# A state-space recurrence handled two chunks at a visit instead of one, between the projections of a hybrid layer

## The chip, the cores and the metric

The kernel runs on one core of a Trainium2 chip. The metric is the device time of one execution in microseconds (us), as the median of several runs. The core has five engines that work side by side: TensorE for matrix products (PE in the profile, with PEld for the loading of its weights), VectorE (DVE), ScalarE (ACT), GpSimd (POOL) and SyncE (SP), which here only issues transfers (DMA). Products land in PSUM, a small memory of eight banks; everything else lies in SBUF, the working memory. A bank holds 512 single-precision numbers for each of 128 partitions.

## The reference

One layer, 1024 positions of 1024 channels, in single precision: a normalisation, one large projection into ten parts, two branches on the parts, gates, an output projection and a last normalisation. The change lies in the first branch, a chunked recurrence (SSD) with 16 heads in 4 groups and chunks of 128 positions, so 8 chunks to a group:

```python
xdt = (xs * dt[..., None]).reshape(bsz, nc, q, g, r, p)
da_cs = jnp.cumsum((dt * a).reshape(bsz, nc, q, g, r), axis=2)
...
decay = jnp.exp(jnp.where(causal[None, None, :, :, None, None], seg, -jnp.inf))
cb = jnp.einsum('bclgn,bcsgn->bclsg', cc, bc)
y_diag = jnp.einsum('bclsgr,bcsgrp->bclgrp', cb[..., None] * decay, xdt)
to_end = jnp.exp(da_cs[:, :, -1:] - da_cs)
states = jnp.einsum('bcsgn,bcsgrp->bcgrpn', bc, xdt * to_end[..., None])
...
def step(carry, inp):
    st, dec = inp
    return carry * dec[..., None, None] + st, carry
...
y_off = jnp.einsum('bclgn,bcgrpn->bclgrp', cc, prev) * jnp.exp(da_cs)[..., None]
y = (y_diag + y_off).reshape(bsz, seqlen, n_heads, p)
```

Within a chunk the output is `y_diag`, a masked product. Across chunks a state of 128 by 64 numbers for each head is carried along, and `y_off` is what the state before a chunk adds to that chunk's output.

## The kernel before

**The stream of projections.** Nearly all of PE's time goes into projections and output products. Each takes two column blocks of weights as a `Pair` (L325 to L460) and computes them by seven products of half size instead of eight, in the manner of Strassen. One such product is a *step*: 12 matmuls of 128 by 128 on 128 by 512, half of which is a *half* (`Stream.half`, L563). The steps of all 48 pairs stand in one fixed list (L501 to L517). For each step, ACT and DVE split the weights into a high and a low part (`split`, L350, which writes the tile `wop`), three steps ahead of the product. Between products 1, 6 and 7 of a pair the partial sum in a bank is copied out by ACT (`keep`, L407), into one of three buffers of the tag `s`, and DVE later adds it to or subtracts it from another product (`give`, L413, at L420, L422 and L424). Products 1, 6, 7 and 4 of a pair add up in one bank (`pb`), so product 4 can't begin before copy 7 is taken.

**The recurrence.** Other work is laid between the halves: a generator does some of it, then yields a number of halves that the stream is to do (`beside`, L638). `ssd(g)` (L850) is the generator of one group's recurrence. Its parts for a chunk `c`:

- `sums(c)` (L855) loads the running sums of the decays, spread over all partitions, into `csb` (128 by 512, two buffers).
- `decays(c)` (L884) makes, on ACT, four clipped differences (L891) and one exponential (L895) into `m4` (`m` in the profile).
- `first(c)` (L861) is two to three transposes and the product `cb`, all into a bank `tr`; from that DVE makes `xdt` (L872) and the causal `cbm` (L877), ACT copies `bn` (L880), and DVE multiplies the decays by `cbm` (L882): the masked decays.
- `more(c)` (L897): on POOL `xe` (L904); the exponential of the sums into a tile `ce` of its own, on ACT (L910), which POOL multiplies by `ct` (L911).
- `second(c)` (L913) is the state's product `st` (two records of 256 columns in the profile, since a single-precision product counts as two), the new state (POOL L925, DVE L929), and the output products into the bank `yps`: for each of two tiles and two heads first the masked decays against `xdt`, then, for c > 0, the scaled `ct` against the state before. These have 64 columns of output; the profile has them as 128*64. After each odd chunk DVE adds the bank to `xs` (L943).

A visit for chunk c (L959 to L978) is `second(c)`, `first(c+1)`, `more(c+1)`, the load for c+3, then 2 halves of the stream, `decays(c+2)`, and 2 more halves.

**What orders the work.** All matmuls, transposes and everything under `pin` stay in the order in which the program writes them, each engine for itself. Other instructions are put in order when the program is built, by a priority that goes by program order and by when their inputs should be there; `tc.high_priority()` moves an instruction up. After that, every engine works strictly through its list. A tile of a tag with n buffers waits, when it is first written, until the tile n before it (of that tag) is read for the last time.

**Other users of the same buffers.** The setup of the decays (`dt_and_f`, L693), the group's gates and norm (`gate_and_norm`, L1007) and its two halves of `squares` (L980) borrow `csb`, `ce` and `m4` between groups. `turn_values` (L824) transposes a part of the attention's values, when at least 2 halves have gone since it was made.

Of the kernel before, what the change touches and what calls it, by code (L numbers as in the profile page):

```python
# [86 lines left out]
def hybrid_layer(ctx: ExitStack, tc, a, out):  # L87
# [237 lines left out]
    class Pair:  # L325
# [7 lines left out]
        def __init__(self, keys, handlers, ops=None, adds=nc.vector):  # L333
            self.keys, self.handlers = keys, handlers
            self.ops = xop if ops is None else ops
            self.adds = adds
            self.raw, self.op, self.prepared = {}, {}, set()
            self.s1, self.sums = None, 0

# [67 lines left out]
        def keep(self, ps):  # L407
            s = wp.tile([P, HALF], F32, tag="s", bufs=3, name="s")
            with tc.high_priority():
                nc.scalar.activation(s, ps, AF.Copy)  # L410
            return s
# [15 lines left out]
        def do(self, which):  # L427
# [4 lines left out]
            if which == 1:  # L432
# [3 lines left out]
                self.k1 = self.keep(self.b)  # L436
# [5 lines left out]
            elif which == 6:  # L442
                yield from self.matmuls(self.b, 6, "-t2", False)
                self.k2 = self.keep(self.b)
            elif which in (5, 7):
# [3 lines left out]
                else:  # L449
                    yield from self.matmuls(self.b, 7, "t3", False)  # L450
                    self.k7 = self.keep(self.b)
# [241 lines left out]
    def dt_and_f():  # L693

        def rows(tag, bufs):
# [4 lines left out]
            sp.tile([P, 4, P], F32, tag="csb", bufs=2, name="t").rearrange("p a b -> p (a b)") for _ in range(2)  # L700
# [62 lines left out]
        fc = [rows("ce", 1), rows("csb", 2)]  # L763
# [86 lines left out]
    def ssd(g):  # L850
# [4 lines left out]
        def sums(c):  # L855

            if c < NT:
                csb = at[c]["csb"] = sp.tile([P, 4, P], F32, tag="csb", bufs=2, name="csb")
                nc.sync.dma_start(csb, cs_dram[hs, c * P : (c + 1) * P].unsqueeze(0).to_broadcast([P, 4, P]))

        def first(c):  # L861
# [14 lines left out]
            cbm = sp.tile([P, P], F32, tag="cbm", bufs=1, name="cbm")  # L876
            nc.vector.tensor_tensor(cbm, tr[:, 3 * P :], tri, ALU.mult)  # L877
            if c < NT - 1:
                bn = s["bn"] = sp.tile([P, P], F32, tag="bn", bufs=1, name="bn")
                nc.scalar.activation(bn, tr[:, 2 * P : 3 * P], AF.Copy)  # L880
            m4 = s["m4"]
            nc.vector.tensor_tensor(m4, m4, cbm.unsqueeze(1).to_broadcast([P, 4, P]), ALU.mult)  # L882

        def decays(c):  # L884

            if c < NT:
                csb = at[c]["csb"]
                m4 = at[c]["m4"] = sp.tile([P, 4, P], F32, tag="m4", bufs=2, name="m4")
                for h in range(4):
                    pin(  # L890
                        nc.scalar.activation(  # L891
                            m4[:, h, :], csb[:, h, :], AF.Relu, scale=-1.0, bias=cscol[:, c, 4 * g + h : 4 * g + h + 1]
                        )
                    )
                pin(nc.scalar.activation(m4, m4, AF.Exp, scale=-1.0))  # L895

        def more(c):  # L897

            cs = slice(c * P, (c + 1) * P)
            s = at[c]  # L900
            if c < NT - 1:
                xe = s["xe"] = sp.tile([P, 4, 64], F32, tag="xe", bufs=1, name="xe")
# [4 lines left out]
                )  # L907
            if c > 0:
# [4 lines left out]
        def second(c, prev, yps):  # L913

            s = at[c]
            new = None
            if c < NT - 1:
                st = pp.tile([P, 4, 64], F32, tag="st", bufs=1, name="st")
                mm(st, s["bn"], s["xe"], start=True, stop=True)
                new = sp.tile([P, 4, 64], F32, tag="prev", bufs=3, name="new")  # L920
                if c == 0:
                    nc.vector.tensor_copy(new, st)
                else:
                    pin(
                        nc.gpsimd.tensor_tensor(  # L925
                            new, prev, cdec[:, c, hs].unsqueeze(2).to_broadcast([P, 4, 64]), ALU.mult
                        )
                    )
                    nc.vector.tensor_tensor(new, new, st, ALU.add)  # L929
            cc = slice((c % 2) * P, (c % 2 + 1) * P)  # L930
            for j in range(2):
                for e in range(2):
                    h = 2 * j + e
                    mm(yps[e * 64 : e * 64 + 64, j, cc], s["xdt"][:, h, :], s["m4"][:, h, :], start=True, stop=(c == 0))
                if c > 0:
                    for e in range(2):
                        h = 2 * j + e
                        mm(yps[e * 64 : e * 64 + 64, j, cc], prev[:, h, :], s["ce"][:, h, :], start=False, stop=True)
            if c % 2 == 1:
                c2 = slice((c - 1) * P, (c + 1) * P)  # L940
                for j in range(2):
                    i = 2 * g + j
                    nc.vector.scalar_tensor_tensor(  # L943
                        xs[j][:, c2], xs[j][:, c2], dsk[:, i : i + 1], yps[:, j, :], ALU.mult, ALU.add
                    )
            return new

        prev = yps = early = None
        sums(0)
        sums(1)  # L950
        yield 2
        decays(0)
        yield 2
        first(0)
        more(0)
        sums(2)
        decays(1)
        yield 4
        for c in range(NT):  # L959
            if c % 2 == 0:  # L960
                yps = pp.tile([P, 2, 2 * P], F32, tag="y", bufs=1, name="yps")
            prev = second(c, prev, yps)
            if c + 1 < NT:
                first(c + 1)
                more(c + 1)
            sums(c + 3)
            if c == 4:
# [4 lines left out]
                next(early)  # L972
            elif early:
                next(early, None)
            turn_values()
# [760 lines left out]
```

## Time and profile before

| | |
|---|---|
| three runs | 1292.45, 1295.67, 1298.04 us; median 1295.67 |
| the profiled execution | 1295.78 us |
| its span, first to last instruction | 1294.1 us |
| granted TensorE clock, mean | 0.997 |
| busy: PE, DVE, ACT, POOL | 1253.6, 1017.4, 794.1, 289.1 us |
| the recurrence of the four groups, in us from the span's start | 130 to 188, 266 to 325, 402 to 464, 545 to 604 |
| DMA: moved, mean rate | 233.59 MB, 181 GB/s |

How to read the lines that follow. A timeline row has the start in us, the length, the engine, the line of the kernel, the operation, the tiles written and read, and how many such instructions the row merges; in brackets stands how long the engine had been idle, and who ended that. A row of a group has a count, then busy time in us, the mean ns of one, and the idle time ahead of it. The end of a matmul is modelled, so neighbouring matmuls overlap in the rows; what PE really takes is read from one start to the next. "raw" is a block of weights, "th" a buffer for results on their way out, "pb", "pc" and "pd" are the banks of the projections.

### The profile page before, as it was taken

Reading aid. Unit: us, or ns where it says so; the run is one execution under the profiler, and the core shown is the slowest. Engines: PE = TensorE matmul, PEld = TensorE weight load, DVE = VectorE, ACT = ScalarE, POOL = GpSimd, SP = SyncE. Lnnn points to the kernel's source line nnn. Section 1 sums busy time; section 2 is a strip of 40 time slices with the busy share of each in tenths; the row PEclk is TensorE's granted clock in tenths of the full one; section 3 lists DMA queues with packets and bytes.
Section 4 is the critical chain, followed back from the end, with each engine's and each line's share of the span. In section 5 each row is a group of like instructions: output and inputs, shape, how many; then the busy total and the mean of one; then the engine's idle time right before and its main releaser. Section 6 shows DMA issues by size and latency. Waiting matters only on the chain. (4 is left out here: it accounts for less than half of the span.)

```text
span 1294.1 us, 21088 instructions
## 1 busy us (share of the span) xinstructions
PE 1253.6 (97%) x7066; PEld 987.1 (76%) x7066; DVE 1017.4 (79%) x1979; ACT 794.1 (61%) x1729; POOL 289.1 (22%) x307
## 2 busy tenths in 40 slices
PE   6999999999999999899999999999999999999997
PEld 4787888788887788688777777777767777678786
DVE  6999888798789879788666666666789778877875
ACT  8745666477556656566556666566677656743754
POOL 0000430034102420143001222222121313246052
PEclk9999999999999999999999999999999999999999
DMA  7332453654463444454464656566687657666932
GB/s 281 102 107 83 144 149 120 199 144 144 128 209 120 146 154 159 126 151 155 164 230 164 212 180 225 191 214 204 220 278 252 220 176 262 222 212 195 363 117 97
DMA packets 154668, 233.59 MB, mean 181 GB/s; under 512 B 17216, under 2 KB 62656, under 8 KB 154560
## 3 DMA queue, kind: packets, MB, share of 16 engines
q1 hardware_dynamic: 142016, 205.53, 50.0%
q0 software_dynamic: 6400, 16.10, 3.3%
q10 hardware_dynamic: 6144, 10.62, 2.2%
q8 instruction: 55, 0.90, 0.3%
q14 instruction: 53, 0.43, 0.1%
HBM read 162.99 MB, written 72.34 MB: 182 GB/s over the span
## 5 line engine op out<-in xcount | busy, mean ns | idle before, releaser
L356 DVE TENSOR_TENSOR wop<-sum,wop 128x512 fp32r<-128x512 f32 x174 | 140.3, 807 | 55.0 <-ACT wop L354 54.4
L354 ACT ACTIVATE wop<-sum 128x512 fp32r<-128x512 f32 x174 | 108.8, 626 | 91.8 <-DVE sum L363 39.0
L1502 ACT ACTIVATE ex<-ex,nm 128x512 f32<-128x512 f32 (+1 forms) x192 | 116.1, 606 | 73.0 <-DVE nm L1498 72.2
L410 ACT ACTIVATE s<-pb 128x512 f32<-128x512 f32 x141 | 83.4, 592 | 95.2 <-PE pb L130 93.1
L356 DVE TENSOR_TENSOR wop<-raw,wop 128x512 fp32r<-128x512 f32 x149 | 107.1, 721 | 33.9 <-ACT wop L354 33.4
L130 PE MATMUL pc<-x3h,wop 128*128 128x512 f32 x384 | 130.2, 397 | 3.2 <-ACT wop L354 2.1
L130 PE MATMUL pb<-x0h,wop 128*128 128x512 f32 x384 | 131.4, 399 | 0.1
L130 PE MATMUL pc<-x2h,wop 128*128 128x512 f32 x384 | 130.2, 398 | 0.0
L130 PE MATMUL pb<-x6h,wop 128*128 128x512 f32 x376 | 127.7, 397 | 1.6 <-ACT s L410 1.6
L130 PE MATMUL pb<-x5h,wop 128*128 128x512 f32 x376 | 127.0, 396 | 1.3 <-ACT s L410 1.3
L130 PE MATMUL pb<-x4h,wop 128*128 128x512 f32 x376 | 127.4, 397 | 0.3 <-DVE wop L356 0.3
L1498 DVE CUSTOM_DVE_ANT_0 ex<-s,fb 128x512 f32<-128x512 f32 (+1 forms) x192 | 96.7, 552 | 23.5 <-PE s L130 23.4
L354 ACT ACTIVATE wop<-raw 128x512 fp32r<-128x512 f32 x151 | 93.8, 623 | 14.8 <-PE pc L130 9.9
L130 PEld LDWEIGHTS pc<-x3h,wop 128*128 128x128 f32 x384 | 72.2, 188 | 20.8 <-ACT wop L354 3.0
L130 PE MATMUL pd<-x1h,wop 128*128 128x512 f32 x264 | 87.7, 393 | 0.0
L130 PEld LDWEIGHTS pb<-x0h,wop 128*128 128x128 f32 x384 | 72.7, 189 | 16.6 <-ACT x0h L1218 0.8
L130 PEld LDWEIGHTS pb<-x6h,wop 128*128 128x128 f32 x376 | 70.7, 188 | 17.8 <-ACT s L410 2.5
L130 PEld LDWEIGHTS pc<-x2h,wop 128*128 128x128 f32 x384 | 72.1, 188 | 15.9 <-DVE u L422 0.6
L130 PEld LDWEIGHTS pb<-x5h,wop 128*128 128x128 f32 x376 | 70.7, 188 | 17.4 <-ACT s L410 2.2
L214 POOL TENSOR_TENSOR wd<-wd 128x256 f32<-128x256 f32 x32 | 32.5, 1015 | 228.6 <-DMA wd<-in_wo 111.0
L130 PEld LDWEIGHTS pb<-x4h,wop 128*128 128x128 f32 x376 | 70.5, 188 | 16.3 <-DVE wop L356 1.1
L130 PE MATMUL s<-k,q 64*128 64x512 f32 (+3 forms) x576 | 74.3, 370 | 4.6 <-DVE p L1520 2.7
(336 smaller groups left out, 3019.7 us busy)
## 6 DMA issues: line engine op xcount, KB each, us to landing
raw<-in_wu SPq DMA_DIRECT2D x128, 256.0 KB, 3.8
csb<-cs_dram SPq DMA_DIRECT2D x32, 256.0 KB, 5.2
fb<-f_dram SPq DMA_DIRECT2D x16, 512.0 KB, 6.4
rb<-st_dram SPq DMA_DIRECT2D x48, 128.0 KB, 3.3
wd<-in_wo SPq DMA_DIRECT2D x40, 128.0 KB, 3.1
xt<-in_x SPq DMA_DIRECT2D x8, 512.0 KB, 5.8
gs_dram<-th ACTq DMA_DIRECT2D x16, 256.0 KB, 3.5
qh_dram<-th SPq DMA_DIRECT2D x16, 256.0 KB, 5.4
```

The costliest lines, as they stand in the source:

```text
L130: return tc.keep_in_program_order(nc.tensor.matmul(*args, **kw))
L214: pin(nc.gpsimd.tensor_tensor(t[out_], t[a_], t[b_], ALU.subtract))
L354: nc.scalar.activation(op[:, 0], src, AF.Copy, scale=sign)
L356: nc.vector.tensor_tensor(op[:, 1], src, op[:, 0], ALU.subtract)
L410: nc.scalar.activation(s, ps, AF.Copy)
L1498: nc.vector.tensor_tensor_reduce(o, s[e][:, 0:w], fb[hp, h][:, e, 0:w], 1.0, 3.0e38, ALU.add, ALU.min, nm)
L1502: pin(nc.scalar.activation(o, o, AF.Exp, scale=-1.0, bias=nm, accum_out=hd.at(hd.sm, i, h, e)))
```

## The change

A visit handles two chunks, so a group has four visits instead of eight.

- `second(v)` computes the output products of chunks 2v and 2v+1 in one go: first the 8 products of masked decays, then the products with the states. The bank is opened once, by the first products.
- `states(v)` is split off from `second`: the state products of both chunks into one bank, then their two new states. They are placed 2 halves ahead of `second(v)`.
- A visit is then `second(v)`, `first` and `xe` for the next two chunks, the load of sums 2v+3, the decays and scaled `ct` of the first next chunk, 2 halves, the same of the other, 2 halves, the mask of the first, 2 halves, the mask of the other and `states(v+1)`, 2 halves, the load of sums 2v+4.
- `ce` is gone: the exponential is written over the sums in `csb`, which has three buffers instead of two.
- `cbm`, `bn` and `xe` get two buffers instead of one.
- The tag `s` (three buffers) becomes `sa` for copies 1 and 7 and `sb` for copy 6, one buffer each; in three places of the last stages a spare buffer from a pool of that stage stands in.
- `turn_values` waits for 4 halves instead of 2. The borrowers of `ce` take `csb`.

The diff, cut to its core:

```diff
-        def keep(self, ps):
-            s = wp.tile([P, HALF], F32, tag="s", bufs=3, name="s")
+        def keep(self, ps, which):
+            place = self.places.get(which, "sb" if which == 6 else "sa")
+            s = place() if callable(place) else wp.tile([P, HALF], F32, tag=place, bufs=1, name="s")
...
-        if turning and turning[0][0] + 2 <= stream.count:
+        if turning and turning[0][0] + 4 <= stream.count:
...
-                csb = at[c]["csb"] = sp.tile([P, 4, P], F32, tag="csb", bufs=2, name="csb")
+                csb = at[c]["csb"] = sp.tile([P, 4, P], F32, tag="csb", bufs=3, name="csb")
...
+        def masked(c):
+            m4 = at[c]["m4"]
+            nc.vector.tensor_tensor(m4, m4, at[c]["cbm"].unsqueeze(1).to_broadcast([P, 4, P]), ALU.mult)
...
             if c > 0:
-                ce = s["ce"] = sp.tile([P, 4, P], F32, tag="ce", bufs=1, name="ce")
-                tc.keep_in_program_order(nc.scalar.activation(ce, s["csb"], AF.Exp))
+                ce = at[c]["csb"]
+                pin(nc.scalar.activation(ce, ce, AF.Exp))
                 pin(nc.gpsimd.tensor_tensor(ce, ce, ct[:, cs].unsqueeze(1).to_broadcast([P, 4, P]), ALU.mult))
...
+        def states(v, prev):
+            st = pp.tile([P, 2, 4, 64], F32, tag="st", bufs=1, name="st")
+            chunks = range(2 * v, 2 * v + 2)
+            before = []
+            for n, c in enumerate(chunks):
+                if c < NT - 1:
+                    mm(st[:, n], at[c]["bn"], at[c]["xe"], start=True, stop=True, skip_group_check=True)
...
+                with tc.high_priority():
+                    if c == 0:
+                        nc.vector.tensor_copy(new, st[:, n])
+                    else:
+                        pin(
+                            nc.gpsimd.tensor_tensor(
+                                new, prev, cdec[:, c, hs].unsqueeze(2).to_broadcast([P, 4, 64]), ALU.mult
+                            )
                         )
+                        nc.vector.tensor_tensor(new, new, st[:, n], ALU.add)
...
+        for v in range(NT // 2):
+            second(v, before)
+            after = [c for c in (2 * v + 2, 2 * v + 3) if c < NT]
+            for c in after:
+                first(c)
+                tails(c)
+            sums(2 * v + 3)
...
+            if after:
+                decays(after[0])
+                more(after[0])
...
+            yield 2
+            if after:
+                decays(after[1])
+                more(after[1])
+            yield 1
+            turn_values()
+            yield 1
+            if after:
+                masked(after[0])
...
+            yield 2
+            if after:
+                masked(after[1])
+                before = states(v + 1, before[2])
             turn_values()
             yield 2
+            sums(2 * v + 4)
```

Ahead of the first visit of a group, the first two chunks are prepared together: both loads, 2 halves, both decays, 2 halves, both `first`, `xe`, masks and scaled `ct`, 3 halves, `states(0)`, 1 half.

More of the change, by code (lines that the diff above doesn't have):

```diff
@@ L936, in second @@
+        def second(v, before):
+            chunks = range(2 * v, 2 * v + 2)
+            yps = pp.tile([P, 2, 2 * P], F32, tag="y", bufs=1, name="yps")
+            for n, c in enumerate(chunks):
+                cc = slice(n * P, n * P + P)
+                for j in range(2):
                     for e in range(2):
                         h = 2 * j + e
[L938 to L945 removed]
@@ L951, in ssd @@
+            c2 = slice(2 * v * P, (2 * v + 2) * P)
+            for j in range(2):
+                i = 2 * g + j
+                nc.vector.scalar_tensor_tensor(
+                    xs[j][:, c2], xs[j][:, c2], dsk[:, i : i + 1], yps[:, j, :], ALU.mult, ALU.add
+                )
+        early = None
+        for c in range(2):
+            sums(c)
         yield 2
-        decays(0)
+        for c in range(2):
+            decays(c)
         yield 2
-        first(0)
-        more(0)
-        sums(2)
@@ L957, in ssd @@
[L957 to L967, printed above, removed]
+        for c in range(2):
+            first(c)
+            tails(c)
+        for c in range(2):
+            masked(c)
+            more(c)
+        sums(2)
```

110 lines of the change are left out of this document (56 added, 54 removed).

## The prediction

> **What bounds the kernel now.** I read the page's shares first, then busy time in the four recurrence stages, then the list of waits, then PE's timeline through one visit of the recurrence.
>
> ```profile
> PE 1253.6 (97%) x7066; PEld 987.1 (76%) x7066; DVE 1017.4 (79%) x1979; ACT 794.1 (61%) x1729; POOL 289.1 (22%) x307
> PEclk9999999999999999999999999999999999999999
> ...
> sum 238.00, PE 235.90 PEld 191.18 DVE 204.58 ACT 156.90 POOL 99.22; mean PE 58.97 PEld 47.79 DVE 51.15 ACT 39.23 POOL 24.80
> ...
> PE tr L133 <- DVE xs L811: 2.6, 1, 2.6
> PE yps L130 <- DVE m L882: 1.9, 2, 1.4
> ```
>
> The sum line adds up the stretches 130 to 188, 266 to 325, 402 to 464 and 545 to 604 us, one for each group's recurrence: PE counts as busy in 235.9 of 238.0 us, DVE in 86%, ACT in 66%. PE sets the pace, at full clock; DVE has little room. Only two waits of PE belong to the recurrence's own data: 1.9 us for the masked decays and 2.6 us for the first transposes of a group. So the change can win little by removing waits. But "busy" hides what PE loses between products, since their ends are modelled; the starts tell it:
>
> ```profile
> 129.32 0.39 PE L130 MATMUL pb<-x5h,wop 128*128 128x512 f32 x1
> 129.55 0.38 PE L133 MATMUL tr<-ident,xs 128*128 128x128 f32 x2
> 129.77 0.27 PE L133 MATMUL tr<-ident,bt 128*128 128x128 f32 x1
> 129.88 0.39 PE L130 MATMUL tr<-ct,bt 128*128 128x128 f32 x2
> 130.02 0.48 PE L130 MATMUL pb<-x0h,wop 128*128 128x512 f32 x1
> 130.34 0.40 PE L130 MATMUL pb<-x0l,wop 128*128 128x512 f32 x1
> ...
> 142.37 0.39 PE L130 MATMUL pd<-x1l,wop 128*128 128x512 f32 x1
> 142.59 0.40 PE L130 MATMUL pd<-x1h,wop 128*128 128x512 f32 x1
> 142.83 0.59 PE L130 MATMUL st<-xe,bn 128*128 128x256 f32 x2
> 143.35 0.44 PE L130 MATMUL yps<-m,xdt 128*64 128x128 f32 x4
> 143.62 0.39 PE L130 MATMUL yps<-ce,new 128*64 128x128 f32 x4
> 143.84 0.39 PE L130 MATMUL yps<-m,xdt 128*64 128x128 f32 x4
> 144.06 0.39 PE L130 MATMUL yps<-ce,new 128*64 128x128 f32 x4
> 144.38 0.44 PE L133 MATMUL tr<-ident,xs 128*128 128x128 f32 x2
> 144.66 0.27 PE L133 MATMUL tr<-ident,bt 128*128 128x128 f32 x1
> 144.77 0.39 PE L130 MATMUL tr<-ct,bt 128*128 128x128 f32 x2
> 144.91 0.49 PE L130 MATMUL pb<-x4h,wop 128*128 128x512 f32 x1
> 145.23 0.40 PE L130 MATMUL pb<-x4l,wop 128*128 128x512 f32 x1
> ```
>
> The upper block is a visit with the transposes alone, the lower a full one: the state's product `st`, the output products `yps` (64 columns wide, "128*64"), the next chunk's transposes. Between projections starts lie 0.22 to 0.23 us apart.
>
> **What one `yps` block costs beyond its work.** Four terms, each a difference of starts.
> - In: the second `st` record starts about 0.21 after the first (0.59 for both, 0.379 for one by the row below), so the two are fed after 0.43; `yps` starts after 0.52. 0.09 lost.
> - First four records of `yps` take 0.27, the next fours 0.22 each. 0.05 lost.
> - Out: the last four take 0.32 until `tr`. 0.10 lost.
> - The first two transposes take 0.28, against 0.22 in the upper block. 0.06 lost.
>
> Together 0.30 us. Going from the last projection into `st` costs 0.24, hardly over 0.23; and from `tr` back to projections both blocks show 0.14 + 0.32, which is the two records' work and one projection, 0.01 over.
>
> ```profile
> L130 PE MATMUL st<-xe,bn 128*128 128x256 f32 x56 | 16.6, 379 | 0.0
> L130 PE MATMUL yps<-m,xdt 128*64 128x128 f32 x256 | 25.8, 285 | 1.9 <-DVE m L882 1.9
> 190.69 0.39 PE L130 MATMUL pb<-x6h,wop 128*128 128x512 f32 x1
> 191.01 0.44 PE L130 MATMUL yps<-m,xdt 128*64 128x128 f32 x4
> ```
>
> **Part 1: fewer blocks.** Eight `yps<-m,xdt` records belong to a chunk, so 256 are 32 blocks. Afterwards a visit handles two chunks: 16 blocks of twice the length, and each product is still there, as many as before. Entered from a projection instead of from `st`, a block costs the same (last rows: 0.32 from projection to `yps`, 0.09 over 0.23). So 16 × 0.30 = 4.8 us go. The bounds: 16 × 0.19 = 3.0 if only in and out are saved, 4.8 if all four terms are. I take 4.8, since all four are seen in the same block. `st` now stands by itself between projections, two chunks' at once: 16 returns at 0.01, +0.2.
>
> The Trainium skill, TensorEngine Tiling (Array Packing), section Tiling Modes, has a rule for it: another tiling mode drains the array, another tile of the same mode doesn't. The trace agrees: the 64-column entries and exits show 0.09 and 0.10. The Trainium skill, TensorE: Matmul & The Clock Gate, Part 2, gives some 128 cycles at 2.4 GHz for a drain; as an estimate 0.05 us, so that 2 × 16 switches would save only 1.7 us and the sum would be 1293.3; the rows have twice that for each, and they decide.
>
> **Part 2: when the operands are due.** Half a step of the projections is 1.36 us (six starts; the rows below have twelve in 2.72).
>
> ```profile
> 147.78 0.39 PE L130 MATMUL pc<-x3h,wop 128*128 128x512 f32 x1
> 150.50 0.59 PE L130 MATMUL st<-xe,bn 128*128 128x256 f32 x2
> ...
> 418.20 0.39 PE L130 MATMUL tr<-ct,bt 128*128 128x128 f32 x2
> 421.38 0.42 DVE L872 TENSOR_TENSOR xdt<-tr,dtn 128x256 f32<-128x256 f32 x1
> 424.72 1.09 DVE L882 TENSOR_TENSOR m<-m,cbm 128x512 f32<-128x512 f32 x1
> 425.96 0.44 PE L130 MATMUL yps<-m,xdt 128*64 128x128 f32 x4 [1.43 <-DVE m L882]
> ```
>
> Two chunks' visit has 8 halves, as two visits of 4 had. Before, mask and product lay 4 halves apart, but the mask had first to wait for transposes, `xdt` and `cbm` on DVE; the last rows show the worst case, a mask 6.5 us after the transposes and 1.43 us of PE idle. Now `xdt`, `cbm` and the decays are made at the visit's start and the second mask is issued 6 halves later, its inputs long there. It has 2 halves (2.72), the two chunks' `st` (4 × 0.21 = 0.85) and half a block (0.44): 4.0 us. DVE's lag shows in `xdt`, which waits for nothing but the transposes: at worst here 421.38 − 418.59 = 2.8 us. With the mask's own 1.09 that makes 3.9: just enough. I count 1.0 of the 1.9 us as gained, and keep 0 and 1.9 as bounds. The 2.6 us for a group's first transposes stay: they wait for the convolution, whose place isn't changed.
>
> The states' chain (POOL's product, DVE's sum, twice in a row) has the same 2.72 us and more: only the first chunk's new state is needed in the next block, and its products stand in that block's second half. The DVE, ACT and POOL instructions are as many as before; ACT's decays and exponentials of two chunks now fall into the first half of a visit, and its second half is free of them.
>
> **Part 3: the sums' loads.** The decays are multiplied in place, so a load into `csb` must wait until `yps` has read the decays there. The third buffer lets the load of the visit's next even chunk run a visit ahead, but that for chunks 5 and 7 of each group (8 loads) starts only once the block is through, and ACT's decays of that chunk stand two halves after the transposes.
>
> ```profile
> DMA to landing us min/median/max: 4.8/5.2/7.2
> 529.98 0.42 ACT L240 ACTIVATE wl<-wd 128x256 fp32r<-128x256 f32 x1 [3.32 <-DMA wd<-in_wo]
> 532.18 0.30 PEld L130 LDWEIGHTS pb<-x4h,wop 128*128 128x128 f32 x2 [0.43 <-DVE wop L356]
> ```
>
> The first row is that of `csb`. From the start of a visit: block 8 × 0.22 + 0.15 = 1.9, so the load lands at 1.9 + 5.2 = 7.1; the decays' place is at 1.9 + 1.1 (10 records of transposes) + 2.7 = 5.7. ACT would stand 1.4 us. ACT's queue holds behind it the splits of coming weights (`wop`) and the copies out of PSUM (`s`). The other rows show what such a hold costs: ACT stood 3.32 us for a load, and PE's weights came 0.43 late. 1.4 us I cost at nothing: the splits are issued three steps (8.2 us) ahead.
>
> **Part 4: the kept sums.** `s` had 3 buffers in turn; now copies 1 and 7 share one, copy 6 has its own.
>
> ```profile
> L410 ACT ACTIVATE s<-pb 128x512 f32<-128x512 f32 x141 | 83.4, 592 | 95.2 <-PE pb L130 93.1
> 363.75 0.60 ACT L410 ACTIVATE s<-pb 128x512 f32<-128x512 f32 x1 [0.86 <-PE pb L130]
> 364.67 0.69 DVE L420 TENSOR_TENSOR th<-pd,s 128x512 f32<-128x512 f32 x1
> 366.27 0.39 PE L130 MATMUL pb<-x6h,wop 128*128 128x512 f32 x1
> ```
>
> Here ACT writes copy 7 at 363.75, while DVE reads copy 1 until 365.36: the copy now waits 1.61 us. PE needs the bank again at 366.27, 1.92 after the copy's old end, so 0.31 is left. Walking the order of products (L505 to L517) through the 141 rows, I find eight such crossings before the attention and one in the last stage, where the bank's next use is four steps off. Cost: 0; were DVE 1 us later still, 0.7 us in each of the eight, some 5.5.
>
> **The sum.** 1295.78 (this execution; its span 1294.1 and 1.7 around it; the median shown is 1295.67, so no correction) − 4.8 + 0.2 − 1.0 = **1290.2 us**. I use 0.5%, about 6.5 us, as what a measurement of this kernel can tell from no change: below 1289.2 is faster, above 1302.1 slower.
>
> **Rivals.**
> - *More waits go.* All 1.9 us at `yps` and the 2.6 at `tr` vanish as the engines' orders shift: 1295.8 − 4.6 − 4.5 = 1286.7. For it: the waits are few and each hangs on DVE's order. Against: nothing moves the convolution.
> - *The kept sums eat it.* Part 4's 5.5 us: 1295.8 − 5.6 + 5.5 = 1295.7, no change. For it: eight crossings, 0.31 left. Against: DVE gives these sums priority.
> - *Slower: the late load.* Should the 8 loads land after 7.2 us (the longest seen), the hold is 9.1 − 5.7 = 3.4 us; past Part 4's 1.92 us of cover that is 1.5 us of PE each, 12 in all: 1290.2 + 12 = 1302.2. It decides from a landing of about 5.7 us on (3.8 + 1.9). Against: a hold of 3.32 cost 0.43. The Trainium skill, TensorE: Matmul & The Clock Gate, table at the head, has ACT's queue as strictly in order, which speaks for this rival; the rows at 529.98 and 532.18 agree that waits pass on, at a small price.
> - *Nothing is saved*, the block's losses being paid by `st` standing alone: 1295.8 − 1.0 = 1294.8. The 0.24 into `st` and 0.01 back speak against it.
>
> **How the numbers follow.** Forecast 0.57, more waits gone 0.16, kept sums 0.13, late load 0.11, nothing saved 0.03. The forecast's own bounds run from 1289.3 (all 1.9 us) to 1293.0 (3.0 us of blocks, no wait), and orders that shift add a few us either way; I put 0.22 of its 0.57 below 1289.2. Faster 0.22 + 0.16 = 0.38; slower 0.10 of the late load's 0.11; the rest, 0.52, is the same. The range reaches down past 1286.7 to 1285 and up to 1299, which takes in the cases without change and half of the way to the late load.
>
> **What would show it.** In the profile after: `yps` in 16 blocks, eight of four records at 0.22 and one entry and exit each; `st` in fours with 0.01 around it; no wait of ACT's decays (L891's like) on `csb` over 2 us; copies of `s` waiting for DVE before 650 us, without PE waiting for `s`. PE's waits in the four stages over 6 us in sum, or the blocks' four losses found unchanged in number, would prove me wrong.

## The result, and the profile after

| | before | after |
|---|---|---|
| median (runs beside each other) | 1296.33 us (4) | 1314.34 us (4) |
| lowest to highest | 1292.45 to 1298.04 | 1312.77 to 1317.13 |
| the profiled execution, its span | 1295.78, 1294.1 | 1317.13, 1315.2 |

The ratio is 1.0139, with a 95% interval of 1.0117 to 1.0160: the change makes the kernel slower by 18 us. 1290.2 us had been forecast, and 1299 was the upper end.

The page's shares and the clock by slices, then what PE waited for in all; these answer to the first lines shown of before.

```profile
PE 1257.9 (96%) x7066; PEld 990.8 (75%) x7066; DVE 1018.1 (77%) x1979; ACT 793.2 (60%) x1729; POOL 287.5 (22%) x307
PEclk9999999999999999989999999999999999999999
...
PE yps L130 <- DVE new L942: 12.8, 9, 3.9
PE tr L133 <- DVE xs L813: 2.7, 1, 2.7
PE yps L130 <- DVE m L899: 1.5, 3, 0.6
PE yps L130 <- DVE new L935: 1.1, 3, 0.4
PE st L130 <- POOL xe L907: 0.9, 1, 0.9
```

Counts and busy times are as they were, but a wait stands on top that before didn't have at all: `yps` for `new`, the states, 13.9 us in 12 waits (the rows of L942 and L935); and the clock has a slice below 9. The mask's wait is 1.5 us (1.9 before), that for a group's first transposes 2.7 (2.6).

From PE's starts, each taken to the next start, I added up four stages: the same steps of the stream in both kernels, from the start of each recurrence until 2 to 8 steps behind its end. They took 96.8, 79.3, 87.2 and 88.1 us before and 102.0, 84.8, 88.9 and 97.3 after: 21.5 more. The rest of the program is the same within 1.2 us, each stretch for itself. Of the 21.5, `yps` has +17.8, projections +6.3, transposes +2.3, `st` −5.0.

Where nothing waits, the block is what the prediction said. PE's timeline around one:

```profile
604.73 0.39 PE L130 MATMUL pc<-x2h,wop 128*128 128x512 f32 x1
605.05 1.09 PE L130 MATMUL yps<-m,xdt 128*64 128x128 f32 x16
605.97 1.04 PE L130 MATMUL yps<-csb,new 128*64 128x128 f32 x16
606.95 0.44 PE L133 MATMUL tr<-ident,xs 128*128 128x128 f32 x2
607.22 0.27 PE L133 MATMUL tr<-ident,bt 128*128 128x128 f32 x1
```

From the projection into `yps` 0.32, as before; 16 records take 0.92 and 0.98 where fours took 0.22: once 0.05 over at the start and once 0.10 over at the end; 0.27 for the first two transposes. One set of losses for 32 records instead of two.

Where it does wait, the rows of all engines between the state products and the block's second half tell how (a visit of the first group, other rows left out):

```profile
149.23 1.03 PE L130 MATMUL st<-xe,bn 128*128 128x256 f32 x4
...
149.90 1.29 POOL L918 TENSOR_TENSOR csb<-csb,ct 128x512 f32<-128x512 f32 x1 [4.64 <-ACT csb L917]
...
151.47 1.44 POOL L918 TENSOR_TENSOR csb<-csb,ct 128x512 f32<-128x512 f32 x1 [0.27 <-ACT csb L917]
...
152.86 1.18 POOL L214 TENSOR_TENSOR wd<-wd 128x256 f32<-128x256 f32 x1
...
153.99 0.61 PE L130 MATMUL yps<-csb,new 128*64 128x128 f32 x8
154.00 0.61 POOL L938 TENSOR_TENSOR new<-new,cdec 128x256 f32<-128x256 f32 x1
154.59 0.69 DVE L364 TENSOR_TENSOR sum<-raw 128x512 f32<-128x512 f32 x1 [1.15 <-DMA raw<-in_wu]
155.20 0.68 DVE L357 TENSOR_TENSOR wop<-raw,wop 128x512 fp32r<-128x512 f32 x1
155.81 0.41 DVE L942 TENSOR_TENSOR new<-new,st 128x256 f32<-128x256 f32 x1
...
156.28 0.66 PE L130 MATMUL yps<-csb,new 128*64 128x128 f32 x8 [1.68 <-DVE new L942]
```

`st` is out at about 150.2, and the old state is long there. But POOL's product L938 stands in its list behind both scaled `ct`, which waited for ACT's exponentials, and behind a difference of weights: it begins at 154.00, when PE is in the block already, and ends at 154.61. Then DVE's sum L942 stands behind a sum of weights (L364) that waits for its load, and behind a split, until 155.81. PE's 8 products with the first chunk's state ran meanwhile; those with the second waited 1.68 us. POOL's waits for those exponentials in the whole execution, before and then after the change (us, times, longest):

```profile
POOL ce L911 <- ACT ce L910: 23.8, 19, 3.1
POOL csb L918 <- ACT csb L917: 49.6, 19, 5.6
```

The longest such wait is in the last group. A row of POOL, two of DVE and one of PE:

```profile
582.71 0.61 POOL L938 TENSOR_TENSOR new<-new,cdec 128x256 f32<-128x256 f32 x1
...
585.65 0.69 DVE L364 TENSOR_TENSOR sum<-raw 128x512 f32<-128x512 f32 x1 [3.50 <-DMA raw<-in_wu]
...
587.20 0.41 DVE L942 TENSOR_TENSOR new<-new,st 128x256 f32<-128x256 f32 x1
...
587.66 1.12 PE L130 MATMUL yps<-csb,new 128*64 128x128 f32 x8 [3.92 <-DVE new L942]
```

Here POOL was through at 583.32, before PE needed the state. DVE stood 3.50 us at a load, with the state's sum three places behind. The nine waits of the row of L942 part in two kinds. In four visits, 8.8 of the 12.8 us, DVE's sum began 1.2 to 3.9 us after POOL's product was through, and a sum of weights that had waited for its load stood two or three places ahead. In the other five, 4.0 us, it began within 0.5 us of POOL's end: there POOL's product came late.

### The profile page after: what moved, and what is told of

The parts are those of the page before. It is cut to its first block, busy times and chain, and to the rows that moved or that the text cites. A ratio compares the mean times of both kernels' runs of the same rounds, so it can differ in the third digit from the quotient of the medians.

```text
span 1315.2 us, 21099 instructions
## 1 busy us (share of the span) xinstructions
PE 1257.9 (96%) x7066; PEld 990.8 (75%) x7066; DVE 1018.1 (77%) x1979; ACT 793.2 (60%) x1729; POOL 287.5 (22%) x307
## 5 line engine op out<-in xcount | busy, mean ns | idle before, releaser
L357 DVE TENSOR_TENSOR wop<-raw,wop 128x512 fp32r<-128x512 f32 x149 | 111.6, 751 | 40.1 <-ACT wop L355 39.9
L130 PEld LDWEIGHTS pb<-x5h,wop 128*128 128x128 f32 x376 | 71.4, 190 | 18.6 <-ACT s L412 3.1
```

The lines of the kernel that those rows point to most:

```text
L130: return tc.keep_in_program_order(nc.tensor.matmul(*args, **kw))
L357: nc.vector.tensor_tensor(op[:, 1], src, op[:, 0], ALU.subtract)
```

## The experiments

Theory: the states are late, because POOL's and DVE's lists hold other work ahead of them, and the change leaves them 2 halves of the stream instead of 4. Rivals: the shared buffers of kept sums; late loads of `csb`. All medians are in us, ratios are to runs of the kernel before on the same chip, with the 95% interval. The executions of e2, e5, e6, e8 and e10 (four or five of each) lie 6 to 10 us apart, so differences of 3 us among these say nothing. e2, e11, e12, e14 and e17 compute something else, with every instruction still there.

| run | median | ratio |
|---|---|---|
| e1_sums_only | 1295.16 | 1.0005 (0.9990 to 1.0019) |
| e2_old_state | 1309.51 | 1.0101 (1.0072 to 1.0129) |
| e3_states_early | 1311.96 | 1.0129 (1.0108 to 1.0150) |
| e4_product_early | 1304.18 | 1.0068 (1.0050 to 1.0085) |
| e5_states_and_product | 1305.01 | 1.0083 (1.0058 to 1.0108) |
| e6_wide_start | 1308.08 | 1.0090 (1.0055 to 1.0124) |
| e7_z_later | 1312.61 | 1.0141 (1.0116 to 1.0165) |
| e8_all | 1305.13 | 1.0072 (1.0047 to 1.0098) |
| e9_values_and_masks | 1310.55 | 1.0118 (1.0097 to 1.0139) |
| e10_late_state_before | 1305.51 | 1.0078 (1.0045 to 1.0112) |
| e11_after_ready_sums | 1292.73 | 0.9969 (0.9954 to 0.9983) |
| e12_e5_ready_sums | 1291.23 | 0.9954 (0.9938 to 0.9970) |
| e13_one_by_one | 1295.95 | 0.9996 (0.9980 to 1.0012) |
| e14_before_ready_sums | 1288.65 | 0.9931 (0.9911 to 0.9952) |
| e15_seven_loads | 1306.60 | 1.0070 (1.0048 to 1.0092) |
| e16_one_by_one_seven | 1297.85 | 1.0010 (0.9994 to 1.0027) |
| e17_one_by_one_ready | 1293.00 | 0.9973 (0.9959 to 0.9988) |
| e18_one_by_one_three_sums | 1295.44 | 0.9990 (0.9976 to 1.0005) |

**Kept sums alone (e1).** The kernel before with Part 4 of the change only:

```diff
-            s = wp.tile([P, HALF], F32, tag="s", bufs=3, name="s")
+            place = self.places.get(which, "sb" if which == 6 else "sa")
+            s = place() if callable(place) else wp.tile([P, HALF], F32, tag=place, bufs=1, name="s")
```

> The kernel before with one part of the change alone: the tag s in place of three buffers has one for copies 1 and 7, one for copy 6 and the spare in the last stages. Late state (the theory: PE waits in the second half of a block for the first next chunk's new state): no change, 1296 +- 3 us, since the recurrence is as before. Shared buffers (the rival): a good part of the 18 us shows up here, 1302 or more, with PE waiting for copies of s.

1.0005: in the kernel before, the shared buffers cost nothing that can be measured, and e18 below shows the same with joined blocks. In the changed kernel itself three buffers were not tried; PE's waits there for the copies are 4.1 us in all, 2.9 before.

**The state taken away (e2).** The changed kernel; from the second visit on, the second chunk's products take the older state.

```diff
-  yps[...], before[n][:, h, :], at[c]["csb"][:, h, :],
+  yps[...], before[n if v == 0 else 0][:, h, :], at[c]["csb"][:, h, :],
```

> The changed kernel, but from the second visit of a group on, the second chunk's output products take the same state as the first chunk's, an older one, so a block doesn't need the state made two halves earlier; that part of the computation is changed, every instruction is still there. Late state: the waits of PE for DVE's new (12.8 us in the changed kernel) are nearly gone, and with them the half clock after the long ones (some 4 us), so 1298 +- 4 us. Shared buffers or late loads: no better than 1310 us.

Only 5 of the 18 us come back. PE's waits for states are down to 2.0 us, but between 125 and 650 us those for ACT's copies out of the bank went up, from 3.0 us in 2 waits after the change (the profiled execution, 1303.68 us, is the fastest of four):

```profile
PE pb L130 <- ACT s L412: 9.8, 7, 2.2
```

So the state is where the lateness is met first; with it gone, another operand is met late. That was a first sign that the cause lies further back.

**State products earlier (e3), POOL's product earlier (e4), both (e5).** In e3 `states(v+1)` stands two halves earlier, ahead of the first mask. In e4 POOL's product of the first new state, which needs only the old state, is issued at the visit's start, ahead of the scaled `ct`. e5 has both.

In e3:

```diff
             if after:
+                before = states(v + 1, before[2])
                 masked(after[0])
...
                 masked(after[1])
-                before = states(v + 1, before[2])
```

and in e4:

```diff
             second(v, before)
             after = [c for c in (2 * v + 2, 2 * v + 3) if c < NT]
+            made = carried(after[0], before[2]) if after else None
...
-                before = states(v + 1, before[2])
+                before = states(v + 1, before[2], made)
```

> The changed kernel with the states' products two halves earlier (ahead of the mask of the first next chunk), so that four halves lie between them and the block that needs the new state. Late state: PE's waits for new fall from 12.8 us to under 4, time 1298 +- 5 us; if what holds the sum is DVE's list behind a late weight load, a wait or two stays. Shared buffers or late loads: within 3 us of 1314.

> The changed kernel with POOL's product of the first next chunk's state (carried state times decay) issued at the start of a visit, ahead of the scaled ct's products, as its inputs are there by then; DVE's sum stays two halves ahead of the block. If POOL's list is what makes the state late: waits for new down by over 8 us, time about 1302. If DVE's list is (the sum stands behind sums of weights that wait for their load): waits down by 4 at most, 1308 to 1314.

> The kernel with the early product (POOL's product for the first new state at the visit's start), and besides the state products two halves earlier, ahead of the first mask. Late state in both lists: the chain then has 4 halves (5.4 us) as before the change, and nothing of POOL stands between; if the 9 us that are left in the stages hang on the state's second half of the chain, the wait for the states (2.0 us) goes and the time falls to some 1301 to 1302 us. Rival, group starts: what is left lies in the first visit of each group, which this edit doesn't touch: 1303 to 1305 us.

e3 gains next to nothing, 2 us, and leaves 11.3 us of waits for states: the matrix product was never the late one. e4 gives back 10 us and leaves 2.0 us of these waits. Its rows for the visit shown above (a difference of weights on POOL, then DVE):

```profile
152.87 1.18 POOL L214 TENSOR_TENSOR wd<-wd 128x256 f32<-128x256 f32 x1
...
153.38 0.41 DVE L953 TENSOR_TENSOR new<-new,st 128x256 f32<-128x256 f32 x1
153.71 0.89 DVE L364 TENSOR_TENSOR sum<-raw 128x512 f32<-128x512 f32 x1
```

With POOL's product early, the planner of the order also put DVE's sum ahead of the sum of weights. So e4 changed both lists, and the 10 us can't be put down to POOL's alone. e5, with 4 halves of lead as before the change, is no faster than e4, and PE waits 0.7 us for states in it: the rest isn't the states.

**The rest sought piece by piece (e6 to e9).** All build on e4: the first visit of a group two halves later (`yield 3` to 4, `yield 1` to 2); the z loads in `squares` four halves later; e5 with both; e5 with the first `turn_values` behind the first mask and the masks under `tc.high_priority()`. Of e6, e7 and e9:

```diff
-        yield 3
+        yield 4
         before = states(0, None)
-        yield 1
+        yield 2
...
-            if early:
+            if early and v > 2:
                 next(early, None)
...
-            yield 1
-            turn_values()
-            yield 1
+            yield 2
             if after:
                 before = states(v + 1, before[2], made)
                 masked(after[0])
+            turn_values()
```

> The kernel with the early product, and besides a group's first visit two halves later: one half more ahead of its state products and one more behind them. Group starts: the first block of each group stands 1.2 to 1.6 us for the second mask and the copied state, 5 to 6 us in the four groups; with 2.72 us more they go, and the time falls by 4 to 5 us to some 1299 to 1300 us. Rival, states or loads: 1303 to 1305 us, unless the later end of each group costs something of its own (then above 1305).

> The kernel with the early product, and besides the loads of the gates z in the third visit of a group four halves later (the work on them follows later by as much). Late loads: SP stands 5.7 us at such a load until the gate is written, and the blocks of weights queue behind it, so that DVE's sums of weights wait and with them all that DVE does for PE; without that hold the bank of transposes is emptied in time (2.3 us), the copies come sooner (3.1 us) and the half-clock stretch that follows in the last group goes (1.7 us): some 1298 to 1300 us. Rival, group starts: the holds are idle time that costs PE little; 1303 to 1305 us.

> The kernel with the early product and all three edits: state products two halves earlier, a group's first visit two halves later, the loads of z four halves later. If waits alone made the change slower, the saving of the fewer blocks (4.6 us) must now show: 1290 to 1294 us against 1295 before the change. If the longer list of work for two chunks costs DVE and ACT time that no order gives back, it stays above 1296 us.

> The kernel with the early product and the early state products, and besides two small moves: the first transposes of values in a visit one half later (behind the first mask), and both masks moved up in DVE's list. Two chunks' burst: what is left (6 us in the four stages against the kernel before, 9 us in the time) is DVE and ACT being late with the first half of a visit, whoever waits for it; the waits at the transposes of values (some 1.5 us over clean) and at the masks (1.9 us) go, and 1301 to 1303 us are left, with copies out of PSUM late in their place. Rival, these two waits alone and what follows them: 1297 to 1299 us.

None gained over e4 and e5. In e6 the first visits' waits for the mask are gone, and others stand in their place (3.3 us at a transpose of the gates, 3.0 at those of values). In e7 the copies, which were to come sooner, were late by 13.4 us instead of the 4.1 of e4; SP stood at the z loads as long as in the changed kernel (29 us between 120 and 630 us), so e7 didn't take that hold away and is no test of it. In e9 the masks, though moved up, were late by 3.6 us instead of the 1.9 of e5. PE's waits in e7:

```profile
PE pb L130 <- ACT s L412: 13.4, 10, 2.9
```

and in e9:

```profile
PE pb L130 <- ACT s L412: 5.9, 7, 2.6
PE yps L130 <- DVE m L900: 3.6, 5, 1.9
PE st L130 <- POOL xe L908: 3.2, 3, 2.0
```

**The lead alone, without two chunks (e10).** The kernel before with the kept sums; the state's part of `second` is moved behind `decays(c+2)`, two halves after the block, with two buffers each for `bn` and `xe`.

```diff
             decays(c + 2)
+            prev = state(c, prev)
             yield 2
```

> The kernel before, one chunk a visit, with the kept sums of the change; the state product, POOL's product and DVE's sum are done two halves behind the block instead of ahead of it, so that a new state has 2 halves instead of 4. Order theory: the scaled ct of one chunk is made at once behind the block and is through when the state's product comes, so that POOL and DVE manage it in 2 halves; PE waits for new states under 3 us in sum, 1295 to 1299 us. Cover theory: two halves are too few whatever stands in POOL's list; 24 visits wait some 0.5 to 1 us each, 1307 us and more.

It lies between the two forecasts, at +9 us. The blocks of `yps` alone took 40.3 us against 31.0 in the kernel before (starts in the four stages); in them PE waited 5.8 us for states and 1.4 for masks. One of the waits, with DVE's rows:

```profile
286.82 0.42 DVE L874 TENSOR_TENSOR xdt<-tr,dtn 128x256 f32<-128x256 f32 x1
287.15 0.28 DVE L879 TENSOR_TENSOR cbm<-tr,tri 128x128 f32<-128x128 f32 x1
287.54 0.94 DVE L884 TENSOR_TENSOR m<-m,cbm 128x512 f32<-128x512 f32 x1
291.70 0.69 DVE L364 TENSOR_TENSOR sum<-raw 128x512 f32<-128x512 f32 x1 [3.23 <-DMA raw<-in_wu]
```

`st` was out at 288, POOL's product at 290.97; the block began at 291.00, and DVE still stood at a load until 291.70; the state's sum followed at 292.31, and PE's products with it came 1.34 us late. So half the lead, with one chunk a visit, costs half of what the change cost. The rows fit a plain reading: a stop of DVE of 3 us is covered by 4 halves (5.4 us) and not by 2 (2.7).

**DVE's stops taken away (e11, e12, e14).** The sum that stands is the first of each pair, of the two blocks loaded last. In these kernels it is made of the two loaded before, so that one operand of two of the seven products is another:

```diff
-                self.s1 = self.total(r["a21"], r["a22"])
+                self.s1 = self.total(r["a11"], r["a12"]) if self.adds is nc.vector else self.total(r["a21"], r["a22"])
```

> The changed kernel, but DVE's first sum of weights of a pair is made of the two blocks that were loaded a pair of loads earlier, so that it never stands at the newest load (this changes what is computed: one operand of two products of seven). DVE stops: DVE idles 21 us in the four stages at these loads with the states' sums behind it; without that the states wait only for POOL, 1306 to 1309 us. POOL alone: 1313 to 1315 us.

> The kernel with the early product and the early state products, with the same sums that never stand at the newest load (changes what is computed in the same way). DVE stops: what is left of the slowing goes, 1291 to 1296 us. Rival, two chunks' work in the first half of a visit: it stays at 1301 to 1305 us.

> The kernel before with the same sums that never stand at the newest load (changes what is computed in the same way): the measure for the two others. Its states have a whole visit, so DVE's stops of 16 us in the stages are covered: 1292 to 1296 us by either theory.

This is the experiment that decides. DVE's waits for these loads between 120 and 630 us, first of the kernel before (us, times, longest):

```profile
DVE sum L363 <- DMA raw<-in_wu: 15.8, 8, 3.7
```

then after the change:

```profile
DVE sum L364 <- DMA raw<-in_wu: 21.2, 11, 3.9
```

In these three kernels the row is gone. The edit does one thing more. Since the operands are there, the planner also puts these sums of weights (0.69 us each) some places earlier in DVE's list; nearly all else there keeps its order between 120 and 630 us in the changed kernel. What the wait is worth and what the place weren't separated; in the four visits above the place can be worth no more than 0.7 us each, of waits of 1.0 to 3.9. The changed kernel gains 21.6 us, far more than forecast, the kernel before 7, also more. Against the same edit in the kernel before, the change costs 4.1 us instead of 18 (1292.73 and 1288.65), and with e5's order 2.6. What is left of the waits for states in e11 is mostly POOL's part, since in all six DVE's sum begins within 0.5 us of the end of POOL's product:

```profile
PE yps L130 <- DVE new L942: 4.8, 6, 1.1
```

So some 14 of the 18 us (from the ratios, 0.9969 over 0.9931 against 1.0139, 13, with about 4 of uncertainty) are DVE standing at loads with work of the recurrence behind it, which the kernel before mostly hides and the changed one doesn't. Of these, 8.8 us were seen above as waits for states; the rest would be copies, transposes and the clock (below), which isn't shown one by one. The 10 us of e4 are no further part beside them: its order moved the state's sum out from behind the same stops.

**Only the blocks joined (e13, e17, e18).** The output products of two chunks in one block, but chunks prepared one by one, 4 halves apart, states made as in the kernel before, `bn`, `xe` and `cbm` single again (shortened: several calls to a line, conditions left out):

```diff
+            before.append(state(2 * v + 1, before[-1]))
+            second(v, before[2 * v : 2 * v + 2])
+            first(c); tails(c); decays(c); more(c); masked(c); sums(c + 1)
...
+            yield 3
+            decays(c + 1)
+            yield 1
+            before.append(state(c, before[-1]))
+            first(c + 1); tails(c + 1); more(c + 1); masked(c + 1); sums(c + 2)
+            yield 4
```

e17 adds the ready sums, e18 the three buffers `s` of the kernel before.

> Only the output products of two chunks are joined: 16 blocks instead of 32, as in the change, but the chunks are prepared one by one, 4 halves apart, and each state is made 4 halves before the next chunk's as in the kernel before (the first of a pair half a visit behind the block, the second just ahead of the block, which needs it only one visit later). No state product stands behind the scaled ct of two chunks, no chunk's decays meet the other's. If fewer blocks are worth what a clean double visit shows (0.28 us each, 4.5 us in all) and lateness alone made the change slow: 1290 to 1292 us. Rival, two chunks in one bank and one visit cost something else that no order gives back (the bank of the outputs, the in-place exponentials, the loads behind the block): 1296 us or more.

> The kernel that joins only the output products and prepares chunk by chunk, with the sums that never stand at the newest load (changes what is computed, as in the three kernels with ready sums). Fewer blocks are worth 0.28 us each once nothing waits: 4 to 5 us below the kernel before with the same sums (1288.7), 1283.5 to 1285.5 us. If the joined block costs something of its own besides waits, 1287 to 1290 us.

> The kernel that joins only the output products and prepares chunk by chunk, with the three buffers in turn for kept sums as in the kernel before (the room that its single xe, bn and cbm leave). Shared kept sums: in the joined kernel copies wait 8.9 us for DVE's sums and PE 6.3 us for copies; with three buffers most of that goes and the blocks' 4 to 5 us show: 1290 to 1292 us, below both kernels. Rival, the copies are late for ACT's own list, whatever their buffers: 1295 to 1297 us, as with the shared ones.

The 14 us of waits for states are gone, and the time is that of before. The saving is there in PE's starts: in the second group of e18 `yps` took 7.16 us, `st` 3.30, `tr` 4.14, against 7.76, 3.67 and 4.38 before, 1.21 less, or 4.8 in four groups, if all went as this one. But the projections of the four stages took 277.1 us against 272.4. In these PE waits 2.2 us for copies of `s`, in the kernel before not at all. The shared buffers aren't the reason, since three buffers changed nothing. In the rows of e18 for the first group, ACT stands at a load of `csb`, the copy is two places behind, and PE waits:

```profile
185.11 1.28 ACT L889 ACTIVATE m<-csb,cscol 128x128 f32<-128x128 f32 x4 [1.72 <-DMA csb<-cs_dram]
186.42 0.63 ACT L893 ACTIVATE m<-m 128x512 f32<-128x512 f32 x1
186.96 0.58 ACT L411 ACTIVATE s<-pb 128x512 f32<-128x512 f32 x1
...
187.59 0.50 PE L130 MATMUL pb<-x6h,wop 128*128 128x512 f32 x1 [0.80 <-ACT s L411]
```

This is one of three such waits, and one more has a load of `csb` ahead of it; a fourth and longer one (2.66 us, between two stages) has ACT behind POOL's differences of weights. 2.2 of the 4.7 us are seen so, and a stretch of 3.41 us at half clock from 541.52 on makes some 1.7 (an estimate: half of it). The rest stays open, and so does why e17, which came out above both of its forecasts, is 4 us above e14.

**A seventh buffer for weights (e15, e16).** The room of the kept sums given to `raw` (7 instead of 6), blocks loaded one at a time.

```diff
-            self.loads = [(p, names) for p in pairs for names in (("a11", "a12"), ("a21", "a22"))]
+            self.loads = [(p, names) for p in pairs for names in (("a11",), ("a12",), ("a21",), ("a22",))]
```

> The kernel before with the kept sums of the change, and the room that they free given to a seventh buffer for blocks of weights; the blocks are loaded one at a time instead of two. If DVE's stops come from loads issued late for want of a buffer, they shrink and most of the 7 us that ready sums gave come without changing what is computed: 1288 to 1292 us. If they come from SP standing at other transfers, 1294 to 1297 us.

> Joined output products, chunks prepared one by one, and the seventh buffer with single loads. If the stops come from late loads for want of a buffer, both gains show: 1284 to 1288 us, below both kernels. If from SP standing elsewhere: 1294 to 1297 us, as with six.

DVE's stops stay (18.6 us in e15, 20.8 in e16), so a want of buffers doesn't make them; e15 is even 9 us slower, with masks late by 5.9 us. What holds the loads isn't settled. SP issues them in order behind the writes and reads of gates: between 120 and 630 us it stood 29 us at the z loads after the change, 15 before. At the loads of `csb` it stood 11 us, 25 before, so these, which now wait for a block, aren't it. No version that computes the same is faster than the kernel before: e13 and e18 have ratios of 0.9996 and 0.9990.

## Why the prediction was wrong

**Part 1 held for the blocks themselves, and showed in no kernel's time.** In the clean group of e18 `yps`, `st` and `tr` lost 0.60, 0.37 and 0.24 us, where four blocks fewer by the prediction's terms make 0.60, 0.36 and 0.24. **Part 4 held** in the kernel before (e1); after the change PE waited 4.1 us for copies, 2.9 before. **Part 3 held in sum**: ACT's waits at `csb` after the change are 0.4 us in the stages, less than the 8 × 1.4 us of the working; the late-load rival is refuted for the change, though the same mechanism showed in e18.

**Part 2 failed**, and with it the sum, which had no term for the states, in this step: "The states' chain (POOL's product, DVE's sum, twice in a row) has the same 2.72 us and more". The lead was compared with what the chain takes when nothing is ahead of it. Three things were left out.

- Each engine works strictly through its list. On POOL the pinned order has the scaled `ct` of both chunks ahead of the product, and these wait for ACT; POOL waited 49.6 us for those exponentials after the change, 23.8 before. The rows at 149.90 show it, and e4, whose edit is to POOL's order. The Trainium skill, TensorE: Matmul & The Clock Gate, table at the head, has the queues of ACT, DVE and POOL strictly in order; these rows agree.
- DVE's lag was read off `xdt` in one place, 2.8 us. The length that counted was that of DVE's longest stop, 3.7 us, for which the trace of before had a row among DVE's waits (above, e11); the prediction quoted PE's waits only. With 5.4 us of lead those stops were covered, with 2.7 not: e5, e10, e11.
- The kernel before already paid 7 us for these stops (e14), which the list of PE's waits doesn't put under that name. In e14 the mask's wait of 1.9 us is gone and that for a group's first transposes is 1.4 us instead of 2.6; where the rest of the 7 was lost isn't shown.

The prediction said that waits of PE over 6 us in the four stages would prove it wrong. They were 16 for states, masks and `xe` alone. The only rival with the other sign named the load of `csb` and ACT; the delay came from the load of weights and DVE, and from POOL's list. The mask, for which the working counted 3.9 of 4.0 us, did not get worse (1.5 us).

The sum by terms, with what was measured: blocks −4.8 (e18); states, for which the sum had nothing, +13.9 of PE's waits; mask −0.4 instead of −1.0; projections +6.3. That makes 15.0, where the stages took 21.5 more; the rest isn't put to a term. The stages have three stretches at half clock, 13.7 us in all, and before none: some 6.8 us by an estimate (half of their length), spread over projections and blocks. One of them, worth 1.7, follows the first transposes of the last group and not a state.

## What to carry to other kernels

When a change moves a producer nearer to its consumer, compare the lead that is left with the longest stop of each engine in the chain (a load, another engine), and read in that engine's list what is queued ahead; the chain's own durations (0.6 and 0.4 us here) are the smallest part. When the removal of one wait makes another grow, stop moving things: find the instruction that stands first in some list and take away what it waits for, if need be by a kernel that computes something else, and give the kernel before the same edit as a measure.

## What the runs showed of the hardware

Waits that are each well below 3.4 us can halve PE's clock for 3.4 us more. The windows of after ahead of and behind two waits (us, then busy time of PE, PEld, DVE, ACT, POOL with counts, then the granted clock and DMA):

```profile
296.70:300.10 3.40, 1.09 (x16) 0.85 (x16) 2.12 (x5) 0.94 (x2) 1.46 (x2) 1.00 0.22 83
300.10:303.50 3.40, 3.20 (x19) 2.87 (x19) 3.37 (x9) 0.00 (x0) 1.10 (x2) 0.50 0.56 169
583.40:586.80 3.40, 0.34 (x8) 0.10 (x2) 1.15 (x2) 0.32 (x1) 0.00 (x0) 1.00 0.42 148
586.80:593.60 6.80, 5.94 (x25) 5.03 (x26) 6.66 (x14) 1.92 (x7) 2.23 (x3) 0.50 0.49 132
```

In the first stretch PE had waited 0.62 us for a mask and then 2.15 us for a state, and was busy for 1.09 of 3.40 us; the clock was 0.50 in the 3.4 us that followed. After the wait of 3.92 us it was 0.50 for 6.8. So two waits of 2.8 us together can cost some 1.7 us again (an estimate: half of 3.4). The Trainium skill, TensorE: Matmul & The Clock Gate, Part 1, has half clock after one or more idle windows of about 3.4 us that run freely. The length of the stretches agrees; that the window must be idle doesn't, since PE worked for a third of the first one. A wait alone doesn't decide it: for the first transposes of the last group PE waited 2.62 us before the change and 2.68 after it; behind the first the clock stayed at 1.00 for 6.8 us, behind the second it was 0.50 from 559.53 on for 3.41 us.
